# Depthwise 3x3 convolution on one core: taps of the last group accumulated in PSUM, diagonals built on two engines

## The chip, the cores and the metric

The kernel runs on one NeuronCore of a Trainium2 chip. The metric is the device time of one execution in microseconds, as the median of several runs. The engines are named as in the profile: PE is TensorE (matmuls; PEld its weight loads), DVE is VectorE, ACT is ScalarE, POOL is GpSimd and SP is SyncE.

## The reference

A depthwise convolution: each of 64 channels has its own 3x3 filter, applied to 16 images of 64x64, without padding. The result is 62x62 for each image and channel.

```python
def reference(x, weight):          # x: 16,64,64,64 f32; weight: 64,1,3,3 f32
    for b in range(batch):
        for c in range(channels):
            output[b, c] = signal.correlate2d(x[b, c], weight[c, 0], mode="valid")
    return output                  # 16,64,62,62 f32
```

## The kernel before

**Layout.** Two images with their 64 channels fill the 128 partitions, so there are eight groups of two images (NG = 8). A group's input is the tile `xb`, 128 x 64 x 64 in bf16; POOL's queue loads it from DRAM and converts it on the way (`issue_load`, L73). Group 0 is loaded in four pieces of rows (0-12, 12-32, 32-48, 48-64), group 1 in two, the others in one. Six `xb` buffers take the loads of the groups ahead.

**Three engines share the nine taps.**
- PE takes six taps, the columns 0 and 2 of the filter (`PE_TAPS`). For each tap a 128x128 diagonal matrix (`diag`) holds the tap's weight of each partition, so a matmul of `diag` with a shifted view of `xb` multiplies each channel by its weight and adds the product up in PSUM (L171).
- DVE takes tap A, the filter's middle column in row 0: one instruction reads PSUM, multiplies a shifted view of `xb` by tap A's weights, adds both and writes the bf16 output tile `sb` (L117). That is called the eviction below.
- ACT takes taps B and C, the middle column in rows 1 and 2: it writes `xwB` (L153) and `xwC` (L158), the shifted input times the weight, in bf16. DVE adds them to `sb` with two more instructions (L133).

**Blocks.** The 62 output rows of a group are two blocks: rows 0-31 in four sub-blocks of 8 rows, and rows 32-61 in sub-blocks of 8, 8, 8 and 6 rows. A block has one PSUM tile (`pt0` or `pt1`, four banks, one for each sub-block). In the profile they carry a running number, and `pt_112` is the first block and `pt_605` the last. A sub-block is six matmuls of 8 x 62 = 496 columns (372 for the sub-block of 6 rows), so a block is 24 matmuls. The PSUM tiles of both names exist once: a block's first matmul waits until the block of the same name in the group before is evicted.

**The start.** The weights come by two small loads on SP's queue. POOL makes the f32 identity `ident`. DVE makes the six diagonals, in the order of the taps, as `ident` times a column of the weights (L88). The first matmul needs diagonal 0 and the first piece of group 0.

**The end.** The groups 0 to 5 are stored with one DMA each (L201), group 6 in two (L196). In the last group each block is evicted in two halves, each with its two L133 adds, and stored in two halves (L184 and L188), all from POOL's queue, in order.

**Order and waits.** The program is written as a loop over groups; a scheduler and the tile framework lay down the order on each engine and the waits. An engine works through its instructions in order.

Of the kernel before, what the change touches and what calls it, by code (L numbers as in the profile page):

```python
# [11 lines left out]
@with_exitstack  # L12
def kernel(
    ctx: ExitStack,
    tc: tile.TileContext,
    x: bass.AP,
    weight: bass.AP,
    out: bass.AP,
):
    nc = tc.nc  # L20
    fp32 = mybir.dt.float32
    bf16 = mybir.dt.bfloat16

    B, C, H, W = x.shape
    _, _, K, _ = weight.shape
    HO = H - K + 1
    WO = W - K + 1

    BPG = 128 // C
    NG = B // BPG  # L30
    P = BPG * C

    def tap_idx(di, dj):
        return di * K + dj

    PE_TAPS = [(0, 0), (1, 0), (2, 0), (0, 2), (1, 2), (2, 2)]
    TAP_A = (0, 1)
    TAP_B = (1, 1)
    TAP_C = (2, 1)

    NT = K * K
    NPE = len(PE_TAPS)

    SB = [
        (0, (8, 8, 8, 8)),
        (32, (8, 8, 8, 6)),
    ]

    const_pool = ctx.enter_context(tc.tile_pool(name="const", bufs=1))
    xbpool = ctx.enter_context(tc.tile_pool(name="xbpool", bufs=PREFETCH + 2))  # L50
    spool = ctx.enter_context(tc.tile_pool(name="spool", bufs=4))
    xwpool = ctx.enter_context(tc.tile_pool(name="xwpool", bufs=6))
    psum_pool = ctx.enter_context(tc.tile_pool(name="psum", bufs=1, space=bass.MemoryType.PSUM))

    x_g = x.rearrange("(g p) c h w -> g (p c) h w", g=NG)
    out_g = out.rearrange("(g p) c h w -> g (p c) h w", g=NG)
    half = P // 2

    xb_tiles = {}

    def issue_load(g):
        if g >= NG or g in xb_tiles:
            return
        xbt = xbpool.tile([P, H, W], bf16, name="xb")
        xb_tiles[g] = xbt
        if g == 0:
            segs = (0, 12, 32, 48, H)
        elif g == 1:
            segs = (0, 32, H)
        else:  # L70
            segs = (0, H)
        for r0, r1 in zip(segs[:-1], segs[1:]):
            nc.gpsimd.dma_start(out=xbt[:, r0:r1], in_=x_g[g, :, r0:r1, :])  # L73

    w_sb = const_pool.tile([P, NT], fp32)
    w_flat = weight.rearrange("c o kh kw -> c (o kh kw)")
    for h in range(BPG):
        nc.sync.dma_start(out=w_sb[h * C : (h + 1) * C, :], in_=w_flat)

    ident = const_pool.tile([P, P], fp32)  # L80
    make_identity(nc, ident)

    issue_load(0)

    diag = const_pool.tile([P, NPE, P], bf16)
    for ti, (di, dj) in enumerate(PE_TAPS):
        t = tap_idx(di, dj)
        nc.vector.tensor_scalar(  # L88
            out=diag[:, ti, :],
            in0=ident,  # L90
            scalar1=w_sb[:, t : t + 1],
            scalar2=None,
            op0=mybir.AluOpType.mult,
        )

    for g in range(1, PREFETCH + 1):
        issue_load(g)

    tA = tap_idx(*TAP_A)
    tB = tap_idx(*TAP_B)  # L100
    tC = tap_idx(*TAP_C)

    def dve_block(sb, xb, pt, bank0, i0, subs):
        rows = sum(subs)
        sb_flat = sb.rearrange("p h w -> p (h w)")
        k = 0
        r0 = i0
        while k < len(subs):
            j = k
            while j < len(subs) and subs[j] == subs[k]:  # L110
                j += 1
            n = j - k
            sr = subs[k]
            pt_v = pt[:, bank0 + k : bank0 + j, : sr * WO].rearrange(
                "p a (r c) -> p a r c", r=sr
            )
            nc.vector.scalar_tensor_tensor(  # L117
                out=sb[:, r0 : r0 + n * sr, :].rearrange(
                    "p (a r) c -> p a r c", a=n
                ),  # L120
                in0=xb[:, r0 + TAP_A[0] : r0 + TAP_A[0] + n * sr,
                       TAP_A[1] : TAP_A[1] + WO].rearrange(
                    "p (a r) c -> p a r c", a=n
                ),
                scalar=w_sb[:, tA : tA + 1],
                in1=pt_v,
                op0=mybir.AluOpType.mult,
                op1=mybir.AluOpType.add,
            )
            r0 += n * sr  # L130
            k = j
        for xw in (dve_block.xwB, dve_block.xwC):
            nc.vector.tensor_tensor(  # L133
                out=sb_flat[:, i0 * WO : (i0 + rows) * WO],
                in0=sb_flat[:, i0 * WO : (i0 + rows) * WO],
                in1=xw.rearrange("p h w -> p (h w)")[:, i0 * WO : (i0 + rows) * WO],
                op=mybir.AluOpType.add,
            )

    for g in range(NG):  # L140
        xb = xb_tiles[g]

        issue_load(g + PREFETCH + 1)

        sb = spool.tile([P, HO, WO], bf16, name="sb")
        xwB = xwpool.tile([P, HO, WO], bf16, name="xwB")
        xwC = xwpool.tile([P, HO, WO], bf16, name="xwC")
        dve_block.xwB = xwB
        dve_block.xwC = xwC

        hseg = (0, 10, 32, 46, HO) if g == 0 else (0, 32, HO)
        for r0, r1 in zip(hseg[:-1], hseg[1:]):
            nc.scalar.mul(  # L153
                out=xwB[:, r0:r1, :],
                in_=xb[:, TAP_B[0] + r0 : TAP_B[0] + r1, TAP_B[1] : TAP_B[1] + WO],
                mul=w_sb[:, tB : tB + 1],
            )
            nc.scalar.mul(  # L158
                out=xwC[:, r0:r1, :],
                in_=xb[:, TAP_C[0] + r0 : TAP_C[0] + r1, TAP_C[1] : TAP_C[1] + WO],  # L160
                mul=w_sb[:, tC : tC + 1],
            )

        last = g == NG - 1
        for si, (i0, subs) in enumerate(SB):
            pt = psum_pool.tile([P, 4, 512], fp32, name=f"pt{si}")

            r0 = i0
            for k, sr in enumerate(subs):
                for ti, (di, dj) in enumerate(PE_TAPS):  # L170
                    nc.tensor.matmul(  # L171
                        out=pt[:, k, : sr * WO],
                        lhsT=diag[:, ti, :],
                        rhs=xb[:, r0 + di : r0 + di + sr, dj : dj + WO],
                        start=(ti == 0),
                        stop=(ti == NPE - 1),
                    )
                r0 += sr

            if last:  # L180
                h1 = subs[0] + subs[1]
                dve_block(sb, xb, pt, 0, i0, subs[:2])
                dve_block(sb, xb, pt, 2, i0 + h1, subs[2:])
                nc.gpsimd.dma_start(  # L184
                    out=out_g[g, :, i0 : i0 + h1, :], in_=sb[:, i0 : i0 + h1]
                )
                h2 = sum(subs)
                nc.gpsimd.dma_start(  # L188
                    out=out_g[g, :, i0 + h1 : i0 + h2, :],
                    in_=sb[:, i0 + h1 : i0 + h2],  # L190
                )
            else:
                dve_block(sb, xb, pt, 0, i0, subs)
                if g == NG - 2:
                    rows = sum(subs)
                    nc.gpsimd.dma_start(  # L196
                        out=out_g[g, :, i0 : i0 + rows, :],
                        in_=sb[:, i0 : i0 + rows],
                    )
                elif si == len(SB) - 1:  # L200
                    nc.gpsimd.dma_start(out=out_g[g, :, :, :], in_=sb)  # L201
# [30 lines left out]
```

## Time and profile before

| what | us |
|---|---|
| median of 6 runs | 97.43 (97.23 to 97.86) |
| the profiled execution's own time | 98.08 |
| span of the profiled execution | 96.0 |
| PE matmuls, 384 | 80.6 busy |
| DVE, 68 instructions | 74.5 busy |
| ACT, 37 instructions | 59.6 busy |
| L133 adds, 36 | 37.6 busy |
| one eviction of a whole block of 1984 columns | 2.28 |
| one L133 add of 1984 columns | 1.19 |
| one L153 or L158 of 1984 columns | 1.94 |

The profile is of one execution. Its span runs from the first to the last instruction, and the execution's own time lies 2.08 us above it; the median is of other executions, without a profile. In the profile's rows, a line of the timeline is: start in us, time covered in us, engine, source line, operation, output and inputs with shapes, how many instructions were merged, and in brackets how long the engine sat idle before and what ended that. A shape such as 128x496 is partitions by elements of a partition. Pieces that are merged overlap, so the time covered is not the duration of one times their number.

### The profile page before, as it was taken

The numbers are of one execution on the slowest core, as the hardware profiler recorded it, in microseconds if no ns is written. First come the engines' busy times: TensorE is split into PE (matmuls) and PEld (weight loads), VectorE is DVE, ScalarE is ACT, GpSimd is POOL, SyncE is SP. The second block draws the span as 40 slices with busy tenths as digits, with TensorE's granted clock in tenths as the row PEclk, the third lists the DMA queues.
The fourth block names the chain that finished last, engine by engine and source line by source line (L and its number), as shares of the span: only waits on it lengthen the run. The fifth ranks groups of instructions, "written<-read, shape, count | busy, mean of one in ns | idle before, by whom it ended". The sixth has DMA issues, their size and how long they took to land.

```text
span 96.0 us, 1014 instructions
## 1 busy us (share of the span) xinstructions
PE 80.6 (84%) x384; PEld 38.1 (40%) x384; DVE 74.5 (78%) x68; ACT 59.6 (62%) x37; POOL 13.6 (14%) x30
## 2 busy tenths in 40 slices
PE   0069999999999999999999999999999999990000
PEld 0022444544454445444544454445444544440000
DVE  0050039998999899989998999899989999999900
ACT  0073999999999999999999999997000000000000
POOL 5972000002100220010000100010002020213220
PEclk9999999999999999999999999999999999999655
DMA  0899999999999999999999999989207986548490
GB/s 1 96 172 194 203 220 225 212 215 218 218 208 218 180 381 424 251 218 390 427 239 237 380 423 436 362 340 416 109 0 301 416 308 225 220 177 281 142 395 1
DMA packets 3620, 24.20 MB, mean 252 GB/s; under 512 B 544, under 2 KB 672, under 8 KB 2080
## 3 DMA queue, kind: packets, MB, share of 16 engines
q0 software_dynamic: 3456, 24.14, 86.5%
q8 instruction: 3, 0.05, 0.2%
q1 hardware_dynamic: 160, 0.00, 0.2%
q14 instruction: 1, 0.01, 0.0%
HBM read 16.78 MB, written 15.75 MB: 339 GB/s over the span
## 4 chain that ended last, share of the span: by engine, by line
issue 78%; POOL 9%; DMA 7%; POOLq 1%
DMA xb<-in_x_dram 7%; POOL out_dram L201 3%; POOL xb L73 2%; POOL out_dram L196 1%; POOL out_dram L184 1%; POOLq L227 1%; POOL out_dram L188 1%; POOL ident masks.py:199 0%; POOL ident masks.py:197 0%; POOLq masks.py:199 0%; POOLq L73 0%; POOLq L201 0%; POOLq L188 0%; POOLq L184 0%; POOLq L196 0%
## 5 line engine op out<-in xcount | busy, mean ns | idle before, releaser
L171 PEld LDWEIGHTS <-diag 128*128 128x128 bf16 x384 | 38.1, 99 | 47.9 <-DVE diag L88 6.3
L153 ACT ACTIVATE xwB<-xb,w_sb 128x1984 bf16<-128x1984 bf16 (+5 forms) x18 | 30.7, 1708 | 1.8 <-DMA xb<-in_x_dram 1.8
L158 ACT ACTIVATE xwC<-xb,w_sb 128x1984 bf16<-128x1984 bf16 (+5 forms) x18 | 30.7, 1706 | 0.0
L133 DVE TENSOR_TENSOR sb<-sb,xwC 128x1984 bf16<-128x1984 bf16 (+3 forms) x18 | 18.8, 1048 | 1.5
L133 DVE TENSOR_TENSOR sb<-sb,xwB 128x1984 bf16<-128x1984 bf16 (+3 forms) x18 | 18.8, 1047 | 1.5
L171 PE MATMUL pt_112<-xb,diag 128*128 128x496 bf16 x24 | 7.8, 492 | 5.7 <-DVE diag L88 5.7
L201 POOL DMA_DIRECT2D out_dram<-sb x6 | 3.2, 534 | 59.1 <-DVE sb L133 36.3
L117 DVE SCALAR_TENSOR_TENSOR sb<-xb,w_sb,pt_112 128x1984 bf16<-128x1984 bf16 x1 | 2.3, 2280 | 7.0 <-PE pt_112 L171 7.0
L73 POOL DMA_DIRECT2D xb<-in_x_dram x12 | 6.5, 566 | 2.4 <-DMA xb<-in_x_dram 2.1
L88 DVE TENSOR_SCALAR diag<-ident,w_sb 128x128 bf16<-128x128 f32 x6 | 1.3, 298 | 5.3 <-DMA w_sb<-in_weight_dram 5.3
L171 PE MATMUL pt_376<-xb,diag 128*128 128x496 bf16 x24 | 5.2, 372 | 0.0
L171 PE MATMUL pt_441<-xb,diag 128*128 128x496 bf16 x24 | 5.2, 373 | 0.0
L171 PE MATMUL pt_179<-xb,diag 128*128 128x496 bf16 x24 | 5.2, 372 | 0.0
L171 PE MATMUL pt_246<-xb,diag 128*128 128x496 bf16 x24 | 5.2, 372 | 0.0
L171 PE MATMUL pt_311<-xb,diag 128*128 128x496 bf16 x24 | 5.2, 372 | 0.0
L171 PE MATMUL pt_506<-xb,diag 128*128 128x496 bf16 x24 | 5.2, 372 | 0.0
L171 PE MATMUL pt_572<-xb,diag 128*128 128x496 bf16 x24 | 5.2, 372 | 0.0
L171 PE MATMUL pt_140<-xb,diag 128*128 128x496 bf16 (+1 forms) x24 | 4.9, 360 | 0.0
L171 PE MATMUL pt_207<-xb,diag 128*128 128x496 bf16 (+1 forms) x24 | 4.9, 360 | 0.0
L171 PE MATMUL pt_274<-xb,diag 128*128 128x496 bf16 (+1 forms) x24 | 4.9, 360 | 0.0
L171 PE MATMUL pt_339<-xb,diag 128*128 128x496 bf16 (+1 forms) x24 | 4.9, 360 | 0.0
L171 PE MATMUL pt_404<-xb,diag 128*128 128x496 bf16 (+1 forms) x24 | 4.9, 360 | 0.0
(28 smaller groups left out, 54.5 us busy)
## 6 DMA issues: line engine op xcount, KB each, us to landing
out_dram<-sb POOLq DMA_DIRECT2D x6, 1922.0 KB, 14.3
xb<-in_x_dram POOLq DMA_DIRECT2D x6, 1024.0 KB, 21.6
out_dram<-sb POOLq DMA_DIRECT2D x3, 496.0 KB, 3.0
xb<-in_x_dram POOLq DMA_DIRECT2D x2, 512.0 KB, 11.0
out_dram<-sb POOLq DMA_DIRECT2D x1, 992.0 KB, 5.1
out_dram<-sb POOLq DMA_DIRECT2D x1, 930.0 KB, 3.9
xb<-in_x_dram POOLq DMA_DIRECT2D x2, 256.0 KB, 7.4
out_dram<-sb POOLq DMA_DIRECT2D x1, 434.0 KB, 2.8
```

The costliest lines, as they stand in the source:

```text
L73: nc.gpsimd.dma_start(out=xbt[:, r0:r1], in_=x_g[g, :, r0:r1, :])
L88: nc.vector.tensor_scalar(out=diag[:, ti, :], in0=ident, scalar1=w_sb[:, t : t + 1], scalar2=None, op0=mybir.AluOpType.mult,)
L117: nc.vector.scalar_tensor_tensor(out=sb[:, r0 : r0 + n * sr, :].rearrange("p (a r) c -> p a r c", a=n), in0=xb[:, r0 + TAP_A[0] : r0 + TAP ...
L133: nc.vector.tensor_tensor(out=sb_flat[:, i0 * WO : (i0 + rows) * WO], in0=sb_flat[:, i0 * WO : (i0 + rows) * WO], in1=xw.rearrange("p h w ...
L153: nc.scalar.mul(out=xwB[:, r0:r1, :], in_=xb[:, TAP_B[0] + r0 : TAP_B[0] + r1, TAP_B[1] : TAP_B[1] + WO], mul=w_sb[:, tB : tB + 1],)
L158: nc.scalar.mul(out=xwC[:, r0:r1, :], in_=xb[:, TAP_C[0] + r0 : TAP_C[0] + r1, TAP_C[1] : TAP_C[1] + WO], mul=w_sb[:, tC : tC + 1],)
L171: nc.tensor.matmul(out=pt[:, k, : sr * WO], lhsT=diag[:, ti, :], rhs=xb[:, r0 + di : r0 + di + sr, dj : dj + WO], start=(ti == 0), stop=(t ...
L184: nc.gpsimd.dma_start(out=out_g[g, :, i0 : i0 + h1, :], in_=sb[:, i0 : i0 + h1])
L188: nc.gpsimd.dma_start(out=out_g[g, :, i0 + h1 : i0 + h2, :], in_=sb[:, i0 + h1 : i0 + h2],)
L196: nc.gpsimd.dma_start(out=out_g[g, :, i0 : i0 + rows, :], in_=sb[:, i0 : i0 + rows],)
L201: nc.gpsimd.dma_start(out=out_g[g, :, :, :], in_=sb)
L227: with _tile.TileContext(nc) as tc:
```

## The change

Three edits:
1. The first piece of group 0's load ends at row 10 instead of 12, and the second begins there.
2. The diagonals 0, 2 and 4 are made on ACT, 1, 3 and 5 on DVE as before. ACT also makes `identb`, a bf16 copy of the identity.
3. In the last group, after the six matmuls of each sub-block, two more multiply `identb` with `xwB` and `xwC`, so that taps B and C are added up in PSUM too. DVE then only evicts (`evac_only`, the same instruction as L117), and the L133 adds of that group are gone. The last block is evicted and stored in three pieces (two sub-blocks, one, one) instead of two halves; the first block of that group in two, as before. Each piece's store stands right behind its eviction.

A function `act_evac_block` is added too, and nothing calls it. In the changed kernel the lines are numbered anew: L91 and L97 are the diagonals on ACT and DVE, L105 `identb`, L235 and L244 the matmuls, L128 and L144 what were L117 and L133, L163 the evictions of the last group, L262, L270 and L275 the stores.

```diff
-            segs = (0, 12, 32, 48, H)
+            segs = (0, 10, 32, 48, H)
...
+    identb = const_pool.tile([P, P], bf16)
+
     diag = const_pool.tile([P, NPE, P], bf16)
     for ti, (di, dj) in enumerate(PE_TAPS):
         t = tap_idx(di, dj)
-        nc.vector.tensor_scalar(
-            out=diag[:, ti, :],
-            in0=ident,
-            scalar1=w_sb[:, t : t + 1],
-            scalar2=None,
-            op0=mybir.AluOpType.mult,
-        )
+        if ti % 2 == 0:
+            nc.scalar.mul(
+                out=diag[:, ti, :],
+                in_=ident,
+                mul=w_sb[:, t : t + 1],
+            )
+        else:
+            nc.vector.tensor_scalar(
+                out=diag[:, ti, :],
+                in0=ident,
+                scalar1=w_sb[:, t : t + 1],
+                scalar2=None,
+                op0=mybir.AluOpType.mult,
+            )
+
+    nc.scalar.copy(out=identb, in_=ident)
...
+    def evac_only(sb, xb, pt, bank0, i0, subs):
...
+            nc.vector.scalar_tensor_tensor(
+                out=sb[:, r0 : r0 + n * sr, :].rearrange("p (a r) c -> p a r c", a=n),
+                in0=xb[:, r0 + TAP_A[0] : r0 + TAP_A[0] + n * sr,
+                       TAP_A[1] : TAP_A[1] + WO].rearrange("p (a r) c -> p a r c", a=n),
+                scalar=w_sb[:, tA : tA + 1],
+                in1=pt_v,
+                op0=mybir.AluOpType.mult,
+                op1=mybir.AluOpType.add,
+            )
...
-                        stop=(ti == NPE - 1),
+                        stop=(ti == NPE - 1) and not last,
                     )
+                if last:
+                    for xi, xw in enumerate((xwB, xwC)):
+                        nc.tensor.matmul(
+                            out=pt[:, k, : sr * WO],
+                            lhsT=identb,
+                            rhs=xw[:, r0 : r0 + sr, :],
+                            start=False,
+                            stop=(xi == 1),
+                        )
                 r0 += sr
 
             if last:
-                h1 = subs[0] + subs[1]
-                dve_block(sb, xb, pt, 0, i0, subs[:2])
-                dve_block(sb, xb, pt, 2, i0 + h1, subs[2:])
-                nc.gpsimd.dma_start(
-                    out=out_g[g, :, i0 : i0 + h1, :], in_=sb[:, i0 : i0 + h1]
-                )
-                h2 = sum(subs)
-                nc.gpsimd.dma_start(
-                    out=out_g[g, :, i0 + h1 : i0 + h2, :],
-                    in_=sb[:, i0 + h1 : i0 + h2],
-                )
+                if si == len(SB) - 1:
+                    pieces = [(0, subs[:2]), (2, subs[2:3]), (3, subs[3:])]
+                else:
+                    pieces = [(0, subs[:2]), (2, subs[2:])]
+                r = i0
+                for bank0, ss in pieces:
+                    n = sum(ss)
+                    evac_only(sb, xb, pt, bank0, r, ss)
+                    nc.gpsimd.dma_start(
+                        out=out_g[g, :, r : r + n, :], in_=sb[:, r : r + n]
+                    )
+                    r += n
```

## The prediction

> **What bounds the kernel now.** I read the page first, for the shares by engine and the forty slices:
>
> ```profile
> PE 80.6 (84%) x384; PEld 38.1 (40%) x384; DVE 74.5 (78%) x68; ACT 59.6 (62%) x37; POOL 13.6 (14%) x30
> ...
> PE   0069999999999999999999999999999999990000
> ...
> DVE  0050039998999899989998999899989999999900
> ```
>
> TensorE is full from the third slice to the 36th, and four slices at the end are without it. So there are three stages: a start until TensorE runs, a middle that TensorE sets, and a tail. The chain of waits puts 78% down to "issue" and helps little; the timeline does better. The start:
>
> ```profile
> 5.28 1.28 ACT L153 ACT_TABLE_LOAD   x1 [5.28 <-DMA w_sb<-in_weight_dram]
> 5.32 1.29 DVE L88 TENSOR_SCALAR diag<-ident,w_sb 128x128 bf16<-128x128 f32 x6 [5.32 <-DMA w_sb<-in_weight_dram]
> 5.66 0.30 PEld L171 LDWEIGHTS <-diag 128*128 128x128 bf16 x2 [5.66 <-DVE diag L88]
> ...
> 6.58 0.81 ACT L153 ACTIVATE xwB<-xb,w_sb 128x620 bf16<-128x620 bf16 x1
> ...
> 8.41 0.11 PEld L171 LDWEIGHTS <-diag 128*128 128x128 bf16 x1 [0.55 <-issue]
> ...
> 10.84 9.21 PEld L171 LDWEIGHTS <-diag 128*128 128x128 bf16 x46 [0.27 <-issue]
> ```
>
> Both engines wait for the weights, which land at 5.3 us. VectorE has the first diagonal ready at 5.62 and TensorE loads it at 5.66. ScalarE spends 5.28 to 6.56 on its table load and runs its first ACTIVATE at 6.58. Thirteen weight loads lie between 5.66 and 10.84, 0.41 us apart; the 46 from 10.84 on are 9.21/46 = 0.20 us apart. So TensorE's pace doubles at 10.84 us (the clock row shows 9 all along there; I go by the pace). The load at 8.41 comes some 0.3 us late: its predecessor's matmul waited for the second piece of x. From then to the end nothing interrupts TensorE. The tail:
>
> ```profile
> 81.47 4.87 PE L171 MATMUL pt_605<-xb,diag 128*128 128x496 bf16 x24
> 81.68 2.41 DVE L117 SCALAR_TENSOR_TENSOR sb<-xb,w_sb,pt_572 128x992 bf16<-128x992 bf16 x2 [0.20 <-PE pt_572 L171]
> ...
> 86.39 1.89 DVE L117 SCALAR_TENSOR_TENSOR sb<-xb,w_sb,pt_605 128x992 bf16<-128x992 bf16 x2
> ...
> 88.78 0.59 DVE L117 SCALAR_TENSOR_TENSOR sb<-xb,w_sb,pt_605 128x372 bf16<-128x372 bf16 x1
> ...
> 90.25 0.53 POOL L184 DMA_DIRECT2D out_dram<-sb  x1 [3.00 <-DVE sb L133]
> 90.51 0.61 DVE L133 TENSOR_TENSOR sb<-sb,xwC 128x868 bf16<-128x868 bf16 x1
> 91.42 0.53 POOL L188 DMA_DIRECT2D out_dram<-sb  x1 [0.64 <-DVE sb L133]
> ```
>
> TensorE ends at 86.35 (0.35 busy in the window from 86 to 87). VectorE then works until 91.12. The last store is issued at 91.42, 0.30 after its add ended. By windows of 0.2 us the last two stores move from about 91.33 to 93.65, at some 410 GB/s without a gap. The span ends at 96.0.
>
> **The start, part by part.** Three of the six diagonals (0, 2, 4) go to ScalarE, and matmul 0 needs diagonal 0. In the listing of the changed program the table load still waits for the weights, so it ends at 6.56 again and the first scaling starts at 6.58. No row has a ScalarE operation of 128 columns. The shapes 1984 (1938 ns), 992 (1107 ns) and 620 (some 803 ns) lie on a line of 0.83 ns per column with 0.29 us fixed: 0.39 us for 128, and 0.30 from one start to the next (0.71 between the starts at 620, which lasts 0.81). An estimate between 0.29 (the fixed part alone) and 0.80 us (the row for 620); the line goes through three rows, so I take it. Diagonal 0 is ready at 6.97, 2 at 7.27, 4 at 7.57; VectorE's three are ready before 6.3. TensorE's first load moves from 5.66 to 7.01, by **1.35 us**, and at 0.41 us each none of the later ones waits again. The 0.3 us stall at 8.41 vanishes, because matmul 6 now comes at 9.6. Cutting the first x piece to 10 rows lets it land earlier, which nobody can use before 7.0; rows 2 to 10 are all that the first sub-block reads.
>
> What does a start 1.35 us later cost at the end? If the pace doubles at 10.84 again, TensorE misses 1.35/0.413 = 3.3 slow matmuls, gets 0.3/0.413 = 0.7 back from the stall, and is 2.6 matmuls behind, which at the fast pace (5.0 us for 24, so 0.208) is **0.55 us**. If the doubling moves with the start (5.18 us after the first load), it is 1.35 - 0.7 x 0.208 = 1.20 us. The bounds are 0 (the table load out of the way) and 2.04 (the doubling a step later, below). I take 0.55, for one row: by windows of 0.1 us the granted clock falls to 0.50 at 89.37, 3.0 us after TensorE ended. A clock that counted from TensorE's own start and stop would need some time after each, and here it took 5.18 after the one and 3.0 after the other; points in time that don't depend on the kernel fit both.
>
> The Trainium skill, "TensorE: Matmul & The Clock Gate", Part 1, says that the clock opens after a busy window of about 3.413 us, and that the windows run freely and don't start with the kernel. This trace agrees on the raster: from 10.84 to 89.37 are 78.53 us, 23.0 windows of 3.413. But the rule speaks against my choice where executions are concerned: with another phase in each, the mean would be the 1.20 of the moving point, and the sum 99.6.
>
> The skill's "ScalarE: Activation LUTs", What ACT_TABLE_LOAD costs, adds some 1.38 us of drain to the 1.28 us load. The trace shows none: the ACTIVATE starts at 6.58, 0.02 after the load's end. By the page TensorE would start 2.73 us later, be 5.9 matmuls behind at 10.84, and the sum would be 99.6 as well; I go by the row.
>
> ScalarE itself: three diagonals and the identity copy end at 7.87. Its first xwC piece now also reads rows of x's second piece, which is there at about 8.4, so it reaches the 1364-column pair at about 9.9 instead of 9.70. That is hidden: VectorE first reads xwB at 15.95, when the rows up to 32 have been done since 12.5, and ScalarE ends its last group at 66.7, 11 us before TensorE reads it.
>
> **The order on POOL.** In the listing the loads of groups 6 and 7 stand ahead of the stores of groups 0 and 1 instead of behind them. The load of group 6 waits for group 0's last eviction (20.6) and can go about 3 us earlier; the store behind it waits for an add that ends at 23 and can't go sooner anyway. A load moves 1.05 MB at some 215 GB/s, so it may hold that store up 4.9 us: issued at 23.4 with at most 17.5 to landing, it would be done by 46. Its reader is VectorE in group 4 at 52.5, where the buffer is used again. Cost nothing; without those 6 us of cover it would be up to 4.9.
>
> **The last group.** Sixteen matmuls are added: fourteen of 496 columns at 0.208 and two of 372 at 0.157 (six in 0.94) are **3.23 us**. The weight loads lie under them, as now. TensorE's end moves to 89.58 plus the lag. Eight adds of L133 go. The eviction of the first half (83.35 to 85.8) and its stores are over long before.
>
> When may VectorE start on the last block? The row at 81.68 answers: VectorE was free at 81.47 and wanted two banks that TensorE had filled by 79, and still waited for the end of all 24 matmuls. The changed program's listing has the same form, one wait at the first of the three evictions and none at the others. So they run after 89.58: 1.80 for those of 992 and 496 (86.39 to 88.19, the start of what follows them) and 0.59 for 372, ending at 92.01. VectorE's tail shrinks from 4.73 to 2.4 us; the end of its work moves by **+0.89**.
>
> Stores: the 992 piece ends at 90.87, is issued at 91.17 instead of 90.25, and the same bytes take the same 2.3 us: +0.92. By the last issue: the third store waits for POOL (0.58 for each issue), goes at 92.39 instead of 91.42: +0.97. Smaller rows in the store may cost more; nothing in the trace splits that off, so I bound it by one more issue, 0.58, and by nothing. I take **+0.95**.
>
> **Sum.** 0.55 + 0.95 = +1.50 us. The profiled execution took 98.08 with a span of 96.0, so 97.5 and 99.6 after it; the same shift on the median 97.43 gives **98.9**.
>
> **Rivals.**
> - The doubling moves with the start: 97.43 + 0.95 + 1.20 = 99.6. For it: six runs within 0.6 us, which a free phase would spread wider. Against it: the 5.18 and 3.0 us above.
> - The start falls too late for the doubling at 10.84, and it comes a step later. The nearest row for a step is the 3.0 us to the clock's fall: another 3.0 x (1 - 0.208/0.413) = 1.49, so 97.43 + 0.95 + 2.04 = 100.4. For it: no row says how much of the 5.18 us ahead of the doubling was needed, and 1.35 of them go. Against it: 3.8 are left, more than the 3.0.
> - The start costs nothing, if the table load doesn't stand in the way: 98.4. Against it: its wait is in the listing.
> - **Faster.** Evictions released bank by bank. Then only the 372 piece follows TensorE: 89.62 + 0.59 + 0.30 is an issue at 90.51; its 190 KB move from 91.59 to 92.05 instead of 93.65, so -1.6 + 0.55, 96.4. It decides once the first eviction of the last block starts before about 88.5. The row at 81.68 speaks against it.
>
> **Chances.** Mine 0.50 (98.6 to 99.3 alone), moving point 0.27, one step later 0.08, free start 0.06, bank by bank 0.04, something unseen 0.05 (0.02 of it no change). About 0.3% is what a measurement of this kernel can tell from none. Range 98.3 to 100.1: it holds mine, the moving point and most of the free start. Faster 0.04, same 0.03, slower 0.93.
>
> **What would show it.** First weight load at 7.0; the pace doubling at 10.8 (mine) or 12.2 (moving); TensorE's end at about 90.1; the first eviction of the last block just after it; last store issued at about 92.9; span 97.5. I am wrong if that eviction starts while TensorE still works, or if the first load stays at 5.7.

## The result, and the profile after

| | us |
|---|---|
| changed kernel, median of 8 runs | 99.55 (99.40 to 100.43) |
| kernel before, median of all 16 runs | 97.81 (97.18 to 98.82) |
| ratio | 1.0198, 95% interval 1.0152 to 1.0244 |
| profiled execution, its own time and span | 100.10 and 98.0 |

The changed kernel is slower by 2.0%. On the 97.43 us from which the forecast was made that is 99.4 us; forecast were 98.9 and 98.3 to 100.1. The ratio leaves out runs more than 1.5% above the fastest of their kernel; in the sessions of the experiments these are runs whose TensorE was late at its full pace (shown below), so I also give means of all spans (before, 73 runs in four sessions: 96.10; changed, 9 runs: 97.72; +1.62, give or take 0.3).

The start, from the timeline of the changed kernel (start, time covered, engine, line, operation, how many, idle time before):

```profile
4.88 1.28 ACT L91 ACT_TABLE_LOAD   x1 [4.88 <-DMA w_sb<-in_weight_dram]
4.92 0.70 DVE L97 TENSOR_SCALAR diag<-ident,w_sb 128x128 bf16<-128x128 f32 x3 [4.92 <-DMA w_sb<-in_weight_dram]
6.17 0.98 ACT L91 ACTIVATE diag<-ident,w_sb 128x128 bf16<-128x128 f32 x3
6.63 0.13 PEld L235 LDWEIGHTS <-diag 128*128 128x128 bf16 x2 [6.63 <-ACT diag L91]
...
11.98 7.99 PEld L235 LDWEIGHTS <-diag 128*128 128x128 bf16 x40 [0.26 <-issue]
```

The weights land at 4.88, 0.40 earlier than in the trace of before. In the row at 11.98 the loads come 0.20 us apart, ahead of it 0.41 (left out here). From the landing TensorE needs 1.75 us to its first load instead of 0.38: the table load, one scaling (391 ns each in the groups by form), the handover. The pace doubles at about 12.0, not at 10.84. The tail:

```profile
84.30 2.41 DVE L163 SCALAR_TENSOR_TENSOR sb<-xb,w_sb,pt_574 128x992 bf16<-128x992 bf16 x2 [1.88 <-PE pt_574 L244]
...
90.22 0.32 PE L244 MATMUL pt_611<-xwC,identb 128*128 128x372 bf16 x1
90.58 2.40 DVE L163 SCALAR_TENSOR_TENSOR sb<-xb,w_sb,pt_611 128x992 bf16<-128x992 bf16 x3 [3.87 <-PE pt_611 L244]
92.13 1.70 POOL L262 DMA_DIRECT2D out_dram<-sb  x3 [4.59 <-DVE sb L163]
```

VectorE sits idle for 3.87 us, although two of the last block's four banks were complete at 87.6, and starts when TensorE is done. The two traces then add up as follows, each number read from the timelines and windows:

| | before | changed | difference |
|---|---|---|---|
| weights land | 5.28 | 4.88 | -0.40 |
| from there to the first weight load | 0.38 | 1.75 | +1.37 |
| first load to TensorE's end | 80.69 | 83.92 | +3.23 |
| TensorE's end to the span's end | 9.65 | 7.45 | -2.20 |
| span | 96.0 | 98.0 | +2.00 |

The third row holds the start's slow stretch too. The last group alone, from its first matmul to TensorE's end, takes 9.90 us before (76.45 to 86.35) and 13.14 here (77.41 to 90.55): +3.24.

### The profile page after: what moved, and what is told of

Read it like the earlier page. It is cut to its first block, busy times and chain, and to the rows that moved or that the text cites. A ratio compares the mean times of both kernels' runs of the same rounds, so it can differ in the third digit from the quotient of the medians.

```text
span 98.0 us, 1037 instructions
## 1 busy us (share of the span) xinstructions
PE 83.9 (86%) x400; PEld 39.8 (41%) x400; DVE 69.3 (71%) x57; ACT 60.6 (62%) x41; POOL 14.1 (14%) x31
## 4 chain that ended last, share of the span: by engine, by line
issue 57%; ACT 27%; POOL 6%; DMA 4%; POOLq 1%; SPq 1%; ACTq 0%
ACT xwB L217 13%; ACT xwC L222 11%; DMA w_sb<-in_weight_dram 4%; POOL out_dram L275 3%; POOL out_dram L262 2%; ACT L91 1%; POOL out_dram L270 1%; ACT diag L91 1%; POOL xb L73 1%; SPq L78 1%; POOLq L301 1%; ACT identb L105 0%; POOLq L262 0%; POOLq L275 0%; ACTq L91 0%
## 5 line engine op out<-in xcount | busy, mean ns | idle before, releaser
L235 PEld LDWEIGHTS <-diag 128*128 128x128 bf16 x384 | 38.2, 100 | 48.7 <-ACT diag L91 6.9
L144 DVE TENSOR_TENSOR sb<-sb,xwC 128x1984 bf16<-128x1984 bf16 (+1 forms) x14 | 16.2, 1161 | 1.5
L144 DVE TENSOR_TENSOR sb<-sb,xwB 128x1984 bf16<-128x1984 bf16 (+1 forms) x14 | 16.2, 1160 | 1.5
L235 PE MATMUL pt_114<-xb,diag 128*128 128x496 bf16 x24 | 7.9, 508 | 6.6 <-ACT diag L91 6.6
L275 POOL DMA_DIRECT2D out_dram<-sb x6 | 3.2, 535 | 40.0 <-DVE sb L144 40.0
L128 DVE SCALAR_TENSOR_TENSOR sb<-xb,w_sb,pt_114 128x1984 bf16<-128x1984 bf16 x1 | 2.3, 2281 | 8.9 <-PE pt_114 L235 8.9
L235 PE MATMUL pt_574<-xb,diag 128*128 128x496 bf16 x24 | 5.7, 372 | 0.0
L235 PE MATMUL pt_611<-xb,diag 128*128 128x496 bf16 (+1 forms) x24 | 5.4, 360 | 0.0
L235 PE MATMUL pt_248<-xb,diag 128*128 128x496 bf16 x24 | 5.2, 372 | 0.0
L235 PE MATMUL pt_313<-xb,diag 128*128 128x496 bf16 x24 | 5.2, 373 | 0.0
L235 PE MATMUL pt_181<-xb,diag 128*128 128x496 bf16 x24 | 5.2, 372 | 0.0
L235 PE MATMUL pt_378<-xb,diag 128*128 128x496 bf16 x24 | 5.2, 372 | 0.0
L235 PE MATMUL pt_443<-xb,diag 128*128 128x496 bf16 x24 | 5.2, 372 | 0.0
L235 PE MATMUL pt_508<-xb,diag 128*128 128x496 bf16 x24 | 5.2, 372 | 0.0
L163 DVE SCALAR_TENSOR_TENSOR sb<-xb,w_sb,pt_611 128x992 bf16<-128x992 bf16 (+2 forms) x3 | 2.4, 856 | 3.9 <-PE pt_611 L244 3.9
L235 PE MATMUL pt_142<-xb,diag 128*128 128x496 bf16 (+1 forms) x24 | 4.9, 360 | 0.0
L235 PE MATMUL pt_209<-xb,diag 128*128 128x496 bf16 (+1 forms) x24 | 4.9, 360 | 0.0
L235 PE MATMUL pt_276<-xb,diag 128*128 128x496 bf16 (+1 forms) x24 | 4.9, 360 | 0.0
L235 PE MATMUL pt_341<-xb,diag 128*128 128x496 bf16 (+1 forms) x24 | 4.9, 360 | 0.0
```

The source lines that it names most:

```text
L128: nc.vector.scalar_tensor_tensor(out=sb[:, r0 : r0 + n * sr, :].rearrange("p (a r) c -> p a r c", a=n), in0=xb[:, r0 + TAP_A[0] : r0 + TAP ...
L144: nc.vector.tensor_tensor(out=sb_flat[:, i0 * WO : (i0 + rows) * WO], in0=sb_flat[:, i0 * WO : (i0 + rows) * WO], in1=xw.rearrange("p h w ...
L163: nc.vector.scalar_tensor_tensor(out=sb[:, r0 : r0 + n * sr, :].rearrange("p (a r) c -> p a r c", a=n), in0=xb[:, r0 + TAP_A[0] : r0 + TAP ...
L235: nc.tensor.matmul(out=pt[:, k, : sr * WO], lhsT=diag[:, ti, :], rhs=xb[:, r0 + di : r0 + di + sr, dj : dj + WO], start=(ti == 0), stop=(t ...
```

## The experiments

Each was timed together with the kernel before. Theory A is the forecast's: the pace doubles at a set point, which a later start doesn't move. Theory B: it moves with the start. Where a mean of all spans is compared, "before" is the 96.10 above; six runs leave some 0.4 us on either side of such a difference, twelve some 0.3.

### One part alone

`e1_start` takes only the start of the change:

```diff
-            segs = (0, 12, 32, 48, H)
+            segs = (0, 10, 32, 48, H)
...
+        if ti % 2 == 0:
+            nc.scalar.mul(out=diag[:, ti, :], in_=ident, mul=w_sb[:, t : t + 1])
+        else:
...
```

> Before, with only the start of the change: diagonals 0, 2, 4 on ScalarE and the first x piece cut at row 10; last group as before. First weight load about 1.35 us after the weights' arrival is later than before (some 1.7 us after them instead of 0.35). Theory A (pace doubles at a set point near 11 us): +0.55 us against before. Theory B (the doubling moves with the start, 5.2 to 5.4 us after the first weight load): +1.2 us. If the whole loss were in the last group: 0. The tail after TensorE's end (9.65 us from there to the span's end before) should be unchanged.

Measured: 1.0111 (1.0054 to 1.0168); mean of all spans 96.55, so +0.45 against before. First load 1.74 us after the weights, as expected; tail 9.7. The trace's pace doubles at 12.05.

`e2_fold` takes only the last group, with the diagonals and `identb` on VectorE:

```diff
-    nc.scalar.copy(out=identb, in_=ident)
+    nc.vector.tensor_copy(out=identb, in_=ident)
```

> Before, with only the last group of the change (identity matmuls, evictions alone, three pieces); all diagonals and the identity copy on VectorE, x pieces as before. Start as before; TensorE 3.23 us longer; VectorE's tail 2.4 instead of 4.73 us; stores 0.9 to 1.0 later after that: +0.95 us against before. If the fold were free and only the start cost: 0. If the smaller stores cost a lot: up to +1.5.

Measured: 1.0131 (1.0069 to 1.0192). In its trace TensorE ends at 89.23 and the span at 96.7, so the tail is 7.47, against 9.65 before: with the 3.23 us of matmuls, 3.23 - 2.18 = +1.05. The fold costs about what was worked out, and smaller stores add 0.1 us at most.

The two parts make +1.1% and +1.3%, together a little more than the +2.0% of the whole; by the means of all spans +0.45 and +0.62, together less than the +1.62. The next section shows why such means differ.

### How late is the full pace?

The runs of the kernel before, timed with e1_start, lie 2.5 us apart (23 runs, 96.62 to 99.14), so I asked what orders them. The granted clock falls in the tail, in the changed kernel here (columns: window, its length, busy time of PE, PEld, DVE, ACT and POOL, granted clock, DMA share, GB/s):

```profile
92.80:93.00 0.20, 0.00 (x0) 0.00 (x0) 0.19 (x1) 0.00 (x0) 0.20 (x1) 1.00 0.00 0
93.00:94.00 1.00, 0.00 (x0) 0.00 (x0) 0.00 (x0) 0.00 (x0) 0.82 (x2) 0.98 0.99 345
```

0.98 as a mean of 1 and 0.5 puts the fall at 93.96. The trace's clock record has the stretch at full clock from 12.04 to 93.96, 81.92 us; before it is 10.86 to 89.37, 78.51. Over the thirteen traces that have such a stretch it is 78.51, 81.92 or 85.33 us: 23, 24 or 25 times 3.413. So doubling and fall lie on one raster, whose step is the same in all kernels and whose place differs from execution to execution. That agrees with the Trainium skill ("TensorE: Matmul & The Clock Gate", Part 1), which has windows of 3.413 us that run freely.

With it every run without matmuls of zeros can be placed, not only the profiled ones: span x (2 x mean clock - 1) is the time of the fall (the mean counts all that is ahead of the fall as full clock), and some whole number of steps before it lies the doubling (the number is taken that lies nearest the line below; the clock's three digits leave 0.1 us). For each kernel the span then follows a line of 0.47 to 0.55 us per us of doubling, and half of its runs lie within 0.11 us of it. A slope of 0.5 is what the two paces give (1 - 0.208/0.413). The choice of the step can't make such a line by itself: a step is worth 1.7 us of span, so runs without any tie to the doubling would lie some 0.4 us off in the median. The "span at 10.7" is that of the line with slope 0.5 there:

| kernel | runs | doubling, lowest to highest | mean | span at 10.7 | mean span |
|---|---|---|---|---|---|
| before | 73 | 8.3 to 14.6 | 10.78 | 96.07 | 96.10 |
| changed | 9 | 10.5 to 12.7 | 11.40 | 97.38 | 97.72 |
| e1_start | 6 | 10.0 to 12.4 | 11.32 | 96.26 | 96.55 |
| e2_fold | 6 | 9.1 to 11.9 | 10.06 | 97.01 | 96.72 |
| e3_halves | 12 | 9.2 to 12.1 | 11.03 | 95.54 | 95.71 |
| e8_table | 12 | 8.0 to 11.6 | 9.72 | 96.75 | 96.29 |
| e9_rows10 | 12 | 8.2 to 11.5 | 9.84 | 95.80 | 95.38 |
| e10_rows24 | 8 | 9.5 to 12.0 | 10.84 | 96.10 | 96.18 |
| e7_lastblock | 6 | 9.5 to 11.6 | 10.41 | 93.61 | 93.45 |
| e11_safe | 6 | 8.3 to 11.7 | 10.36 | 93.51 | 93.27 |

One run of before, with a span of 98.2, lies at 14.6; its other 72 end at 12.7.

So most of the spread between runs of a kernel is the doubling's place. The 1.62 us between the changed kernel and before are 1.31 at an equal doubling (97.38 - 96.07) and 0.31 for a doubling that is 0.62 later in the mean. At an equal doubling e2_fold is at +0.94 and e1_start at +0.19, together +1.13. That leaves 0.2 us of the 1.31 unaccounted for.

### What starts the full pace

`e4_warm` gives TensorE work while it would be idle. `e5_warm_before` does the same with nine matmuls in the kernel before.

```diff
+    wz = const_pool.tile([P, 512], bf16)
+    nc.vector.memset(wz, 0.0)
+    warm = psum_pool.tile([P, 4, 512], fp32, name="pt1")
+    for i in range(12):
+        nc.tensor.matmul(
+            out=warm[:, i % 4, :], lhsT=wz[:, :P], rhs=wz, start=True, stop=True
+        )
```

> The changed kernel with twelve 512-column matmuls of zeros ahead of the first real one, from about 1 us on, while TensorE would be idle; their result is read by nobody. Theory (the pace doubles after some 3 to 7 us of TensorE activity, whatever it works on): the real matmuls run at 0.208 from the start or soon after it, 1.3 to 2.6 us less than the changed kernel, so -0.9 to +0.5 against before, and less spread between runs. If the doubling depends on something else (the loads, a set time after launch): as the changed kernel, +1.7 to +1.9.

> The kernel before with nine 512-column matmuls of zeros ahead of the first real one (1.2 to at most 5.1 us), while TensorE would be idle; nobody reads their result. Theory (any TensorE activity starts the time to the doubling): the real matmuls run 0.208 apart from the start, until the seventh, which waits for the second x piece at about 8.4; against an average doubling near 10.6 that is 1.0 to 1.5 us less than before. The later start of the changed kernel then costs nothing (it waits for the same piece), so this one should lie 0.9 to 1.1 under the changed kernel with such matmuls (span 95.5), which is the price of the fold alone. Rival (the doubling doesn't come from activity): same as before. The run with a pace of 0.83 throughout may come again.

Measured: e4_warm 1.0011 (0.9975 to 1.0047) against before, so 1.8% under the changed kernel, with ten of twelve spans between 95.3 and 95.7 (of the others, one 96.1 and one of another kind, see the end). e5_warm_before 0.9870 (0.9803 to 0.9936); by the means of all spans it is 0.64 us under e4_warm (that one run left out), where 0.9 to 1.1 were expected. The trace of e4_warm is that odd run, so the start is shown from e5_warm_before:

```profile
1.20 3.60 PE L89 MATMUL pt<-wz 128*128 128x512 bf16 x9 [1.20 <-DVE wz L86]
...
5.71 1.17 PEld L179 LDWEIGHTS <-diag 128*128 128x128 bf16 x7 [1.41 <-DVE diag L96]
5.72 1.44 PE L179 MATMUL pt<-xb,diag 128*128 128x496 bf16 x6 [0.92 <-DVE diag L96]
...
8.91 4.34 PE L179 MATMUL pt<-xb,diag 128*128 128x496 bf16 x20 [1.76 <-DMA xb<-in_x_dram]
```

Seven weight loads in 1.17 us is the full pace from the start; here the clock record begins at 4.24, 3.04 us after the first matmul of zeros. TensorE's own activity opens the clock, even on zeros. And with the pace there, the second x piece becomes the bound: 1.76 us of waiting until 8.91. A point that no start can move, as theory A has it, doesn't fit that.

### What makes the start late

`e8_table` puts a small multiplication on ScalarE ahead of everything in the changed kernel:

```diff
+    one = const_pool.tile([P, 8], fp32)
+    nc.vector.memset(one, 1.0)
+    one_b = const_pool.tile([P, 8], fp32)
+    nc.scalar.mul(out=one_b, in_=one, mul=one[:, 0:1])
```

> The changed kernel with one ScalarE multiplication of eight ones ahead of everything, so that the table load runs before the weights land. Theory (1.28 of the 1.37 us by which the first weight load is later are the table load): first weight load 0.45 to 0.5 us after the weights instead of 1.75; the cost of the start vanishes: by theory A 0.5 to 0.6 under the changed kernel, by theory B 1.2 under it; what is left against before is the fold, 0.95 to 1.05. If ScalarE is late for another reason: as the changed kernel.

```profile
0.74 1.28 ACT L78 ACT_TABLE_LOAD   x1 [0.74 <-PEq L295]
...
4.89 0.98 ACT L96 ACTIVATE diag<-ident,w_sb 128x128 bf16<-128x128 f32 x3 [2.56 <-DMA w_sb<-in_weight_dram]
...
5.35 0.13 PEld L240 LDWEIGHTS <-diag 128*128 128x128 bf16 x2 [5.35 <-ACT diag L96]
```

With the table load at 0.74 the first load follows the weights by 0.46 us instead of 1.75. 1.0032 (0.9986 to 1.0078), so 1.6% under the changed kernel; by the means of all spans 1.43 less, 0.63 of it at an equal doubling, the rest an earlier one (mean 9.72 instead of 11.40). The 0.63 are what theory A allows for; with the earlier doubling, which A rules out, it is theory B's size. One thing besides the table load differs: on POOL the loads of groups 6 and 7 stand behind the stores again, as in the kernel before. No wait in the changed kernel's trace shows a cost of that order.

Then why does e1_start cost only 0.45? Because it holds a second edit. `e9_rows10` is the kernel before with the first x piece cut at row 10, `e10_rows24` the same with 24:

```diff
-            segs = (0, 12, 32, 48, H)
+            segs = (0, 10, 32, 48, H)
```

> The kernel before with the first x piece cut at row 10, and nothing else. In the five traces so far with 10 rows the weights landed at 4.73 to 5.26 us, in the five with 12 rows at 5.28 to 5.81. Theory C (the weights' small packets share the DMA engines with the first x piece, and fewer rows let them through sooner): landing near 4.9. TensorE then starts some 0.4 us earlier but still waits for the second piece at about 8.4, so the time stays within 0.3 us of before at an equal doubling point. Rival (chance of the execution): landing near 5.4.

> The same with the first x piece of 24 rows, a dose for theory C: if the weights wait behind the piece's bytes, they land 1 to 3 us later than with 12 rows (6.3 or more), and TensorE's first load follows. If the weights don't depend on it: 4.7 to 5.8 as in all the others, and only the first matmul is later, since the larger piece lands later.

Measured: e9_rows10 0.9916 (0.9875 to 0.9957), mean span 95.38, 0.72 under before, where nothing was expected. e10_rows24 1.0041 (0.9984 to 1.0097). The weights' landing in both, in this order, and two weight loads of the first:

```profile
5.10 1.29 DVE L88 TENSOR_SCALAR diag<-ident,w_sb 128x128 bf16<-128x128 f32 x6 [5.10 <-DMA w_sb<-in_weight_dram]
5.61 0.17 PEld L171 LDWEIGHTS <-diag 128*128 128x128 bf16 x2 [5.61 <-DVE diag L88]
...
8.48 0.15 PEld L171 LDWEIGHTS <-diag 128*128 128x128 bf16 x1 [0.26 <-issue]
```

```profile
5.74 1.27 DVE L88 TENSOR_SCALAR diag<-ident,w_sb 128x128 bf16<-128x128 f32 x6 [5.74 <-DMA w_sb<-in_weight_dram]
```

Over all traces they land at 4.7 to 5.3 us with 10 rows (eight traces), 5.3 to 5.8 with 12 (five) and 5.7 with 24 (one). So the weights come earlier with 10 rows, but not as theory C had it: 24 rows should have brought 6.3 or more. An x packet is a partition's rows, 1280, 1536 or 3072 bytes in bf16 (rows x 64 x 2), so the weights' packets may stand behind one x packet each; that is argued, not shown. In e9_rows10 the doubling comes 0.94 earlier in the mean, which is some 0.47 of the gain, and 0.27 is left at an equal doubling. How the earlier weights bring this about isn't shown: in its own trace they land 0.22 before those of before, but the first scaling took 449 ns and the first load comes at 5.61, only 0.05 earlier. What that trace does show is that the stall at 8.41 is gone (8.48, 0.26 after the load ahead of it, as all others). e1_start minus e9_rows10 is 1.17, give or take 0.5: the price of the three diagonals on ScalarE without what the shorter piece gives back.

### What holds the last evictions

`e3_halves` is the changed kernel with PSUM tiles of two banks:

```diff
-            pt = psum_pool.tile([P, 4, 512], fp32, name=f"pt{si}")
+            pta = psum_pool.tile([P, 2, 512], fp32, name=f"pt{si}a")
+            ptb = psum_pool.tile([P, 2, 512], fp32, name=f"pt{si}b")
...
-                        out=pt[:, k, : sr * WO],
+                        out=(pta, ptb)[k // 2][:, k % 2, : sr * WO],
```

> The changed kernel with each block's PSUM in two tiles of two banks, so that a half is released when its own matmuls are done; evictions of all groups in two halves. Theory (the wait for the whole block holds the last evictions): in the last block the first half (1.17 us of VectorE) is evicted while TensorE works, only 496 and 372 columns are left after it; the end comes 1.1 to 1.8 us earlier than in the changed kernel, so +0.1 to +0.8 against before. If the stores alone set the end: within 0.3 of the changed kernel (+1.7 to +1.9).

```profile
87.51 1.25 DVE L165 SCALAR_TENSOR_TENSOR sb<-xb,w_sb,pt1a 128x992 bf16<-128x992 bf16 x1 [2.10 <-PE pt1a L247]
...
90.09 0.32 PE L247 MATMUL pt1b<-xwC,identb 128*128 128x372 bf16 x1
90.45 1.24 DVE L165 SCALAR_TENSOR_TENSOR sb<-xb,w_sb,pt1b 128x496 bf16<-128x496 bf16 x2 [1.69 <-PE pt1b L247]
91.47 1.05 POOL L265 DMA_DIRECT2D out_dram<-sb  x2 [1.89 <-DVE sb L165]
```

The first half goes at 87.51, while TensorE works until 90.41, and the tail is 5.69 instead of 7.45. 1.0002 (0.9957 to 1.0046) against before, and 1.84 us under the changed kernel at an equal doubling, 1.76 of it in the tail. The whole-block wait was worth more than the fold's entire loss.

### Versions that are faster than both

`e7_lastblock` folds in the last block alone, with halves, and leaves the block ahead of it to VectorE's adds; start as before. `e11_safe` adds the first piece of 10 rows. `e6_best` adds to e7_lastblock nine matmuls of zeros and cuts the second x piece in two; `e12_all` has its pieces at rows 10 and 20.

```diff
+            fold = last and si == len(SB) - 1
...
-                if last:
+                if fold:
...
-            segs = (0, 12, 32, 48, H)
+            segs = (0, 12, 22, 32, 48, H)
```

> The fold in the last block alone (eight identity matmuls, 1.56 us), the block ahead of it with VectorE's adds as before; PSUM in tiles of two banks; diagonals and x pieces as before. Theory (whole-block release and adds after TensorE's end made the tail): TensorE ends 1.56 us later, VectorE has evicted the first half by then and ends 1.24 us after TensorE instead of 4.77; last store issued about 1.8 earlier: 1.5 to 2.0 us less than before. Rival (the stores set the end): 0 to 0.6 less.

> The last-block fold with released halves, plus the nine matmuls of zeros at the start, plus the second x piece cut in two (rows 12-22 and 22-32), so that the seventh matmul need not wait until 8.4. If the three gains add up: 1.7 for the tail, 1.1 for the pace, 0.5 to 1.0 for the piece: 3 to 4 us less than before. If the smaller pieces land no earlier: 2.5 to 3.

> The last-block fold with released halves and all diagonals on VectorE, plus the first x piece cut at row 10; no matmuls of zeros. If the gains measured apart (2.5% and 0.8%) add up: 3.0 to 3.5% less than before, median near 94.8. If the earlier start is eaten by the wait for the second piece: as the last-block fold without it, 2.5%.

> The fastest so far (last-block fold, nine matmuls of zeros, second x piece cut) with its first pieces at rows 10 and 20 instead of 12 and 22. If the weights land 0.4 us sooner again: 4.5 to 5.5% less than before. It also shows whether the pace of 0.83 us seen in one execution with such matmuls comes again.

| kernel | median | ratio to before (95% interval) |
|---|---|---|
| e7_lastblock | 95.41 | 0.9748 (0.9698 to 0.9798) |
| e11_safe | 95.46 | 0.9715 (0.9644 to 0.9785) |
| e6_best | 93.81 | 0.9549 (0.9493 to 0.9604) |
| e12_all | 93.51 | 0.9560 (0.9510 to 0.9610) |

In e7_lastblock VectorE is busy with the adds of the block ahead while TensorE does the eight identity matmuls, and little is left after it:

```profile
85.15 1.24 DVE L158 SCALAR_TENSOR_TENSOR sb<-xb,w_sb,pt1a 128x992 bf16<-128x992 bf16 x1
...
87.65 1.25 DVE L158 SCALAR_TENSOR_TENSOR sb<-xb,w_sb,pt1b 128x496 bf16<-128x496 bf16 x2 [1.26 <-PE pt1b L241]
88.68 1.06 POOL L256 DMA_DIRECT2D out_dram<-sb  x2 [1.46 <-DVE sb L158]
```

At an equal doubling it is 2.46 under before, more than the 1.5 to 2.0 expected. What the smaller PSUM tiles would gain in the kernel before without any fold was not run, so the fold's own share of this is open. e6_best, at 4.12 under before by the means of all spans, also gains more than the 3 to 4 expected. In it the start no longer waits:

```profile
6.18 6.81 PEld L240 LDWEIGHTS <-diag 128*128 128x128 bf16 x34 [1.87 <-DVE diag L98]
```

34 loads in 6.81 us are the full pace without a break, although the weights landed late there, at 5.8. The gain of the 10 rows doesn't add to the others within the intervals: 0.3% in e11_safe, where 0.5 to 1.0% were expected, and none in e12_all. In e11_safe's trace TensorE waited for the second piece until 8.49, in e12_all's for another piece until 8.44.

## Why the prediction was right, and where it was not

Direction and order of size were right, and so was most of the mechanism: the fold, the release of the whole block and the table load ahead of the first matmul. The place of the doubling was not. The forecast was +1.50, the ratio says +1.93 (1.48 to 2.38, on 97.43), the means of all runs +1.62. By the ratio the 99.4 lies just outside the 98.6 to 99.3 given for the forecast alone and nearer to the 99.6 of the rival that moves the doubling.

- **TensorE's 3.23 us:** right (9.90 to 13.14 for the last group). That first load to end also gives 3.23 (80.69 to 83.92) is partly chance, since the slow stretch differs a little too: 5.18 us in one trace, 5.35 in the other, without the stall.
- **The whole-block release:** right, from the row at 81.68 of the trace before. e3_halves shows its price.
- **The tail, +0.95:** 1.05 by e2_fold's trace. The last issue came 2.75 us after TensorE's end (92.13 + 1.70 - 0.53 = 93.30) where 2.81 were forecast. The 0.1 lies behind it: from the last issue to the span's end are 4.58 us before, 4.7 here and in e2_fold.
- **The first load, +1.35 after the weights:** 1.37. The scaling was 391 ns against 0.39 worked out, and the table load did the rest, with no drain behind it (ScalarE's first scaling starts at 6.17, 0.01 after the load's end).
- **"I take 0.55", because the pace would double at 10.84 again:** wrong. That point belonged to one execution; in the changed kernel's trace the clock record begins at 12.04. The step of the raster is the same in all traces, but its place varies, and which of its points is taken depends on TensorE's activity. The six runs within 0.6 us, on which the prediction judged the spread, were a narrow draw: 23 runs of the same kernel lie 2.5 us apart. The price of the later start is theory B's: 1.17 (e1_start less e9_rows10) to 1.43 (the changed kernel less e8_table), each give or take 0.5, against the 1.20 forecast for the moving point.
- **"lets it land earlier, which nobody can use before 7.0":** wrong. In the traces with the shorter piece the weights land earlier as well, by some 0.4 us, and alone it gains 0.72 by the means of all spans. By which path is not shown in full.
- The two errors nearly cancel: start as measured +0.45 (e1_start, give or take 0.4), forecast +0.55. So the sum was right by some luck, and the range by the rival that was kept in it.
- **POOL's order:** the loads stand ahead of the stores in the changed kernel and in e1_start, not in e2_fold, e9_rows10 or e8_table, so the diagonals on ScalarE move them and one more ScalarE operation moves them back. No row of the changed kernel's waits shows VectorE held by a late store. It cost nothing that the trace shows, as forecast.

## What to carry to other kernels

Before work is moved off the engine that ends last, look at what releases it: here the adds taken from VectorE came back as idle time, because one PSUM tile covered the whole block; two smaller tiles were worth more than the fold cost. ScalarE's first operation carried a load of 1.28 us here, and if its result starts the critical engine, something trivial should call that load early. And one trace fixes only one throw of the clock: a forecast needs the spread of the runs, which here came to half of each microsecond by which the full pace was late.

## What the runs showed of the hardware

The doubling lay anywhere from 8.0 to 12.7 us after the start in kernels without early matmuls, in one run at 14.6, and 2.7 to 3.4 us after the first matmul of zeros in the three traces with them that have a clock record (4.24, 4.63 and 3.90, from 1.20).

One execution of e4_warm out of twelve, the profiled one, ran at a quarter of the pace throughout:

```profile
1.19 9.94 PE L89 MATMUL pt<-wz 128*128 128x512 bf16 x12 [1.19 <-DVE wz L86]
...
10.82 9.85 PE L243 MATMUL pt<-xb,diag 128*128 128x496 bf16 x12
```

Twelve matmuls in 9.9 us are 0.83 each, four times 0.208, and the span was 326.8 us; the clock row shows full clock there. The Trainium skill, "TensorE: Matmul & The Clock Gate", Part 1, Seeing it yourself, warns of a clock seen stuck at a quarter for 50 us and more, and of clock records that can't be fully trusted; this one lasted for the whole execution. None of the other 29 executions with such matmuls showed it, nor any without. Whether they bring it on is open, and with it whether e6_best and e12_all should be used; e11_safe has none of them.
